# A residual encoder block on one core: x arrives transposed from the host, and the RMS roots are applied behind the projections

## The chip, the cores and the metric

One Trainium2 chip, one core. The time is device microseconds of one execution of the whole kernel. Before the change three runs took 2588.66, 2595.15 and 2600.83 us, median 2595.15 us. One further execution was profiled; all rows come from that one.

## What is computed

x has 2048 rows (frames) of 1024 channels, in f32. The part that matters here is the head of the layer:

```
n = x * rsqrt(mean(x*x, axis=-1) + 1e-6) * g_mix
z = n @ w_in + b_in          # columns: q | k | v | u | B | C | gate_attn | gate_conv
```

q, k and v (512 columns each, 8 heads of 64) go into a chunked attention with a per-head RMS norm; u, B and C go into a short causal convolution; the two gates scale the projections of both. The sum goes through `w_o` and is added to x. Then come a mixture of 32 experts and a gated embedding, which the change does not touch.

The root `r = rsqrt(mean(x*x) + 1e-6)` is one number for each row of x, and `g_mix` one for each channel. So `n @ W` is also `r * (x @ (g_mix * W))`.

## The kernel before, in words

Every matmul runs in three products: each operand is split into a high part (fp32r, a cast on ACT) and a low part (the difference, on DVE or POOL), and `mm3` (L85) issues high x high, high x low and low x high (L93, L94, L95). The helper `split` (L81) is the cast at L82 and the subtraction at L83. `split_scaled` (L479) does the same for `scale * raw`: ACT's scaled copy at L484, DVE's scalar_tensor_tensor at L485.

**Stage 1** (`stage1`, L130) makes q, k, v and the attention. It has 32 tiles of projection work: g = 0 and 1 (four heads each) times t = 0 to 15 (128 rows each). For each g the eight chunks of `w_in` (128x768 each, `load_w`, L163) are loaded and split once. A tile is worked on in three steps:

- `fetch` (L198) issues on SP's queue the load of the tile into `xt` (three buffers): from x for g = 0, from the DRAM buffer `NTd` for g = 1.
- `pre` (L209) makes the stationary operand `nh`, `nl`, that is the normalised tile with its channels on the partitions. For g = 0 it squares the tile on ACT (L219), makes the root on POOL (`rstd`, L126 and L127), multiplies by root and `gmix` on DVE (L222), turns the tile with eight 128x128 transposes on PE (L227) into two PSUM banks, copies them to `nraw` on ACT (L233), stores `nraw` to `NTd` (SP's queue, L234) and splits it (L238 on ACT, L239 on POOL, or on DVE for the first NV = 4 tiles). For g = 1 the turned tile comes back from `NTd` and is only split.
- `proj` (L242) is a generator of pieces: 24 matmuls of 512 columns into one bank (q and k), 24 of 256 columns into another (v), the bias added on DVE out of PSUM (L255, L274), the per-head norm, and the transposes of k and q (L290, L297).

The attention units (one head of one row tile: `score`, `turn`, `scale`, `pv`) are laid between those pieces by a loop written out by hand (L405 to L429): one piece of projection, one unit. `lead=11` pieces run before the first unit. `load_nb` (L184) loads a bias table for each head of g (`nbias`, five buffers).

**Stage 2** (`stage2`, L495) begins inside that loop when the projection pieces are used up, and runs its first pieces between the last attention units. It works in four blocks of 512 rows. For a block `load_n` (L545) brings eight slices of `NTd` (128x512 each) on ACT's queue into `nraw` (two buffers) and splits each into `nh`, `nl` (eight buffers): DMA, ACT cast (L82), DVE subtraction (L83). These are the moving operand of `conv` (u, C, B) and `gate`; weights come in chunks of 128x1024 through `chunk` (L487), split two chunks ahead. `out_proj` ends the block. The blocks after the first load their slices while `out_proj` of the block before runs.

The order of instructions on each engine is fixed when the kernel is built: the framework puts them in order by a simulated schedule, within the priorities of the program text.

Of the kernel before, what the change touches and what calls it, by code (L numbers as in the profile page):

```python
# [18 lines left out]
S = 2048  # L19
D = 1024  # L20
# [52 lines left out]
def bcast_rows(ap_row, n=128):  # L73
    return bass.AP(tensor=ap_row.tensor, offset=ap_row.offset, ap=[[0, n]] + [list(x) for x in ap_row.ap])


class K:
# [21 lines left out]
    def setup(self, ctx):  # L99
        tc, nc, a = self.tc, self.nc, self.a  # L100
        self.cst = c = ctx.enter_context(tc.tile_pool(name="cst", bufs=1))
        self.dr = d = ctx.enter_context(tc.tile_pool(name="dr", bufs=1, space=DRAM))
        self.ident = c.tile([128, 128], F32, name="ident")
        make_identity(nc, self.ident)
        self.identr = c.tile([128, 128], F32R, name="identr")
        nc.vector.tensor_copy(self.identr, self.ident)
        self.H = d.tile([S, D], F32, name="H")
        self.N2 = d.tile([S, D], F32, name="N2")
        self.Y = d.tile([2 * S + (NE + MAXOV) * CAP, D], F32, name="Y")
        self.PP = d.tile([S, D], F32, name="PP")  # L110
        self.mhalf = c.tile([128, 8], F32, name="mhalf")
        nc.vector.memset(self.mhalf, -0.5)
        self.NTd = d.tile([128, 8, S], F32, name="NTd")
        self.YAT = d.tile([128, 4, S], F32, name="YAT")
        self.banks, self.nbank = [], 0

        c.tile([128, 24], F32, name="pad")
# [12 lines left out]
    def stage1(self, outer, after, lead=11, lag=2):  # L130
        tc, nc, a = self.tc, self.nc, self.a
        with ExitStack() as ctx:
# [4 lines left out]
            pj = pjx.enter_context(tc.tile_pool(name="s1proj", bufs=2, side="right", reuse_waits="tile"))  # L137

            bank = self.bank
            gmix = pj.tile([128, D], F32, name="gmix", bufs=1)  # L140
            gqk = pj.tile([128, 8, HD], F32, name="gqk", bufs=1)
            gq = pj.tile([128, 2, HD], F32, name="gq", bufs=1)
            nc.scalar.dma_start(gmix, bcast_rows(a["g_mix"][0]))
            warm = pj.tile([128, 1], F32, name="ss")
            nc.scalar.activation(warm, self.mhalf[:, 0:1], AF.Square)


            early = att.tile([128, 4, 1024], F32, name="KT", bufs=1)
            early_n = att.tile([128, 6, 256], F32, name="PTh1", bufs=1)
            KT, PTh, PTl = [], [], []  # L150

            def tables():
# [5 lines left out]
                        nc.gpsimd.memset(p[:, 5, 0:128].bitcast(F32), 0.0)  # L158
                        P.append(p)

            W, NB, BQ, NS, QT, V, X, YT = {}, {}, {}, {}, {}, {}, {}, {}

            def load_w(g, ks):  # L163
                b = a["w_in"]
                for k in ks:
                    if g == 0:
                        raw = early[:, k - 4, 0:768] if k > 3 else att.tile([128, D], F32, name="QT", bufs=4)[:, 0:768]
                    else:
                        raw = pj.tile([128, D], F32, name="xt", bufs=3)[:, 0:768]
                    self.wlast = nc.sync.dma_start(raw.rearrange("p (s c) -> p s c", c=256),  # L170
                                      bass.AP(tensor=b.tensor, offset=b.offset + k * 128 * 5120 + g * 256,
                                              ap=[[5120, 128], [512, 3], [1, 256]]))
                    wh = pj.tile([128, 768], F32R, name="wh", bufs=8)
                    wl = pj.tile([128, 768], F32R, name="wl", bufs=8)
                    self.split(raw, wh, wl)
                    W[g, k] = (wh, wl)

            def load_bias(g):
# [4 lines left out]

            def load_nb(g, h):  # L184
                E = a["rel_ext"]
                nb = att.tile([128, 640], F32, name="nbias", bufs=5)
                with tc.issue_after(self.wlast.ins):
                    nc.sync.dma_start(nb, E[4 * g + h])
                if g == 0:
# [7 lines left out]

            def fetch(g, t):  # L198
                x = pj.tile([128, D], F32, name="xt", bufs=3)
                if g == 0:  # L200
                    nc.sync.dma_start(x, a["x"][0, t * 128:(t + 1) * 128, :])
                else:
                    nc.sync.dma_start(x.rearrange("p (k c) -> p k c", c=128), self.NTd[:, :, t * 128:(t + 1) * 128])
                X[g, t] = x

            def pool(g, t):
                return nc.vector if g == 0 and t < NV else nc.gpsimd

            def pre(g, t):  # L209
                x = X.pop((g, t))  # L210
                nh = pj.tile([128, 8, 128], F32R, name="nh")
                nl = pj.tile([128, 8, 128], F32R, name="nl")
                if g == 0:
                    if t == 0:
                        nraw = early_n[:, 0:4, :].rearrange("p a (b c) -> p (a b) c", c=128)
                    else:
                        nraw = pj.tile([128, 8, 128], F32, name="nraw", bufs=1)
                    ss = pj.tile([128, 1], F32, name="ss")
                    nc.scalar.activation(nl.rearrange("p a b -> p (a b)"), x, AF.Square, accum_out=ss)  # L219
                    rr = pj.tile([128, 1], F32, name="rr")  # L220
                    self.rstd(rr, ss, D)
                    nc.vector.scalar_tensor_tensor(x, x, rr, gmix, op0=ALU.mult, op1=ALU.mult)  # L222
                    for hf in range(2):
                        tp = bank()
                        for k in range(4):
                            kk = 4 * hf + k
                            nc.tensor.transpose(tp[:, k * 128:(k + 1) * 128], x[:, kk * 128:(kk + 1) * 128], self.ident)  # L227
                        sl = slice(4 * hf, 4 * hf + 4)
                        if t == 0:
                            tv = tp.rearrange("p (k c) -> p k c", c=128)  # L230
                            nc.scalar.copy(nh[:, sl], tv)  # L231
                            nc.vector.tensor_sub(nl[:, sl], tv, nh[:, sl].bitcast(F32))  # L232
                        nc.scalar.copy(nraw[:, sl, :], tp)  # L233
                    nc.sync.dma_start(self.NTd[:, :, t * 128:(t + 1) * 128], nraw)  # L234
                else:
                    nraw = x.rearrange("p (k c) -> p k c", c=128)
                if g or t:
                    nc.scalar.copy(nh, nraw)  # L238
                    pool(g, t).tensor_tensor(nl, nraw, nh.bitcast(F32), op=ALU.subtract)  # L239
                NS[g, t] = [(nh[:, k, :], nl[:, k, :]) for k in range(8)]  # L240

            def proj(g, t):  # L242
# [4 lines left out]
                for half in range(2):  # L247
# [4 lines left out]
                    if half == 0:  # L252
                        yield
                zqk = pj.tile([128, 8, HD], F32, name="zqk", bufs=3)
                nc.vector.tensor_add(zqk, pqk.rearrange("p (h d) -> p h d", d=HD),  # L255
                                     BQ[g][:, 0:2, :].rearrange("p s (h d) -> p (s h) d", d=HD))
                sqk = pj.tile([128, 8, HD], F32, name="sqk")
                pool(g, t).tensor_tensor(sqk, zqk, zqk, op=ALU.mult)
                yield
# [11 lines left out]
                pool(g, t).tensor_tensor(zg, zn, gqk, op=ALU.mult)  # L271
                yield
                zv = pj.tile([128, 4, HD], F32, name="zv", bufs=1)
                nc.vector.tensor_add(zv, pv[:, 0:256].rearrange("p (h d) -> p h d", d=HD),  # L274
                                     BQ[g][:, 2, :].rearrange("p (h d) -> p h d", d=HD))
                Vt = att.tile([128, 4, 2, HD], F32R, name="Vt", bufs=8)
                V[g, t] = Vt
                nc.scalar.copy(Vt[:, :, 0, :], zv)
# [24 lines left out]
            def pieces():  # L303
                fetch(*tiles[0])
                load_w(0, range(WX))
                fetch(*tiles[1])
                load_w(0, range(WX, 8))
                load_bias(0)
                nc.sync.dma_start(gq[:, 0], bcast_rows(a["g_q"][0]))
                nc.sync.dma_start(gq[:, 1], bcast_rows(a["g_k"][0]))  # L310
# [7 lines left out]
                while n < 4 * len(tiles) or live:  # L318
# [5 lines left out]
                            live.remove(p)  # L324
                    if r == 0 and i + 2 < len(tiles):
                        fetch(*tiles[i + 2])
                    if r == 1 and i + 1 < len(tiles):
                        pre(*tiles[i + 1])
                    n += 1
# [165 lines left out]
    def stage2(self, outer, inner):  # L495
# [30 lines left out]
        with ExitStack() as ctx:  # L526
# [12 lines left out]
            tr = rt.tile([128, 512], F32, name="nraw")  # L539
            nc.scalar.dma_start(tr[:, 0:256], a["tri"])  # L540
            nc.gpsimd.tensor_copy(self.tri, tr[:, 0:256])
            halo = small[:, 44:52].rearrange("p (c j) -> p c j", j=2)
            nc.gpsimd.memset(halo, 0.0)

            def load_n(b):  # L545
                out = []
                for k in range(8):
                    raw = rt.tile([128, 512], F32, name="nraw")
                    nc.scalar.dma_start(raw, self.NTd[:, k, 512 * b:512 * b + 512])
                    hi = rt.tile([128, 512], F32R, name="nh", bufs=8)  # L550
                    lo = rt.tile([128, 512], F32R, name="nl", bufs=8)
                    self.split(raw, hi, lo)
                    out.append((hi, lo))
                return out
# [918 lines left out]
def layout(inputs):  # L1473
# [3 lines left out]

    w13 = np.stack([np.asarray(inputs[n])[0].reshape(NE, 8, 128, 4, 128) for n in ("w1", "w3")])
    arrays["w13"] = np.ascontiguousarray(w13.transpose(1, 4, 0, 3, 2, 5)).reshape(NE, 1024, 1024)
    arrays["cst"] = constants()  # L1480
    arrays["tri"] = triangle()
    return arrays
# [15 lines left out]
```

## Time and profile before

| what | value |
|---|---|
| median of three runs | 2595.15 us (2588.66 to 2600.83) |
| the profiled execution | 2593.1 us, of which its span is 2591.3 us |
| mean granted TensorE clock | 0.992 of full speed |
| stage 1 | from 0 to about 560 us |
| stage 2 | from about 560 us to about 1540 us (first and last block overlap their neighbours) |

The 1.8 us between the profiled time and its span lie outside what the profile shows. The profiled execution is 2.05 us below the median of the runs.

### The profile page before, as it was taken

What the parts mean: (1) busy time and instruction counts of PE and PEld (TensorE: products, weight loads), DVE (VectorE), ACT (ScalarE), POOL (GpSimd) and SP (SyncE); (2) the same over time, 40 slices, a digit from 0 to 9 for tenths busy, and PEclk for the clock granted to TensorE, in tenths of its full rate; (3) what the DMA queues carried; (4) which work ended last, traced back from release to release, by engine and by line L of the source; (5) the groups of instructions that cost most, each with busy time, mean ns of one, the idle gap of its engine ahead of it and who ended that gap; (6) DMA issues with size and microseconds to landing.
All of it is one profiled execution on the core that took longest, in us unless ns stands there. A gap on an engine that the chain in (4) does not pass through costs nothing.

```text
span 2591.3 us, 38162 instructions
## 1 busy us (share of the span) xinstructions
PE 2530.0 (98%) x13933; PEld 2191.1 (85%) x13933; DVE 1709.1 (66%) x2745; ACT 1348.1 (52%) x2188; POOL 557.9 (22%) x568
## 2 busy tenths in 40 slices
PE   7999999999999999999999999999999999998998
PEld 6888888888888888888888887998989898986887
DVE  7788867786445444544444445788889888886544
ACT  5666655664333333333333233677777777775322
POOL 2566465520000010001000001111111111111222
PEclk9999999999999999999999999999999999999999
DMA  5212311033536333533353344789999989998452
GB/s 190 73 54 72 109 51 41 14 95 104 154 95 204 120 98 110 199 112 93 121 184 109 98 148 167 267 315 338 324 321 335 335 317 337 335 336 290 157 182 101
DMA packets 331168, 460.47 MB, mean 178 GB/s; under 512 B 26352, under 2 KB 222192, under 8 KB 330976
## 3 DMA queue, kind: packets, MB, share of 16 engines
q1 hardware_dynamic: 297536, 388.35, 45.0%
q0 software_dynamic: 11040, 38.21, 3.9%
q10 hardware_dynamic: 22400, 31.42, 3.7%
q8 instruction: 111, 1.82, 0.3%
q14 instruction: 81, 0.66, 0.1%
HBM read 397.93 MB, written 60.00 MB: 177 GB/s over the span
## 4 chain that ended last, share of the span: by engine, by line
PE 89%; DVE 5%; DMA 3%; ACT 1%; issue 1%; POOL 1%; SPq 0%; ACTq 0%; POOLq 0%; DVEq 0%
PE acc L93 21%; PE acc L95 21%; PE acc L94 21%; PE acc L1079 8%; PE acc L1080 3%; PE acc L1151 2%; PE big L351 2%; PE big L381 2%; PE acc L394 1%; PE acc L395 1%; PE acc L685 1%; PE acc L1049 1%; DMA wraw<-w 1%; DMA h<-H 1%; PE acc L297 1%
## 5 line engine op out<-in xcount | busy, mean ns | idle before, releaser
L83 DVE TENSOR_TENSOR wlo<-wraw,whi 128x1024 fp32r<-128x1024 f32 x560 | 717.0, 1285 | 398.4 <-ACT whi L82 385.3
L82 ACT CAST whi<-wraw 128x1024 fp32r<-128x1024 f32 x560 | 588.5, 1053 | 742.0 <-PE acc L94 376.8
L93 PE MATMUL acc<-nh,whi 128*128 128x512 f32 x896 | 349.8, 392 | 1.9 <-ACT nh L82 1.9
L94 PE MATMUL acc<-nl,whi 128*128 128x512 f32 x896 | 350.0, 391 | 0.0
L95 PE MATMUL acc<-nh,wlo 128*128 128x512 f32 x896 | 348.8, 389 | 0.0
L1079 PE MATMUL acc<-x,whi 128*128 128x320 f32 (+5 forms) x1088 | 289.2, 351 | 1.4 <-DVE x L1062 1.4
L1080 PE MATMUL acc<-x,wlo 128*128 128x160 f32 (+5 forms) x1088 | 258.8, 238 | 0.0
L1080 PEld LDWEIGHTS acc<-x,wlo 128*128 128x128 f32 x1088 | 209.7, 193 | 0.1
L1079 PEld LDWEIGHTS acc<-x,whi 128*128 128x128 f32 x1088 | 206.0, 189 | 1.8 <-DVE x L1062 1.5
L93 PEld LDWEIGHTS acc<-nh,whi 128*128 128x128 f32 x896 | 168.1, 188 | 37.0 <-ACT nh L82 2.6
L95 PEld LDWEIGHTS acc<-nh,wlo 128*128 128x128 f32 x896 | 168.3, 188 | 34.5
L94 PEld LDWEIGHTS acc<-nl,whi 128*128 128x128 f32 x896 | 168.4, 188 | 33.4
L94 PE MATMUL acc<-wl,nh 128*128 128x256 f32 (+1 forms) x512 | 174.5, 342 | 2.5 <-DVE wl L83 2.5
L93 PE MATMUL acc<-wh,nh 128*128 128x512 f32 (+1 forms) x512 | 176.8, 346 | 0.0
L95 PE MATMUL acc<-wh,nl 128*128 128x256 f32 (+1 forms) x512 | 175.2, 343 | 0.0
L610 POOL TENSOR_TENSOR sa<-sa,sc 128x512 f32<-128x512 f32 x32 | 41.2, 1288 | 538.3 <-DVE sc L609 493.3
L386 ACT CAST PTh<-big 128x640 fp32r<-128x640 f32 (+4 forms) x128 | 80.3, 627 | 87.5 <-PE big L381 86.2
L369 ACT ACTIVATE L<-L,four 128x640 f32<-128x640 f32 (+4 forms) x128 | 98.4, 769 | 37.8 <-DVE four L368 15.1
L387 DVE TENSOR_TENSOR PTl<-big,PTh 128x640 fp32r<-128x640 f32 (+4 forms) x128 | 94.0, 735 | 27.6 <-ACT PTh L386 27.1
L94 PEld LDWEIGHTS acc<-wl,nh 128*128 128x128 f32 x512 | 98.5, 192 | 12.4 <-DVE wl L83 3.5
L95 PEld LDWEIGHTS acc<-wh,nl 128*128 128x128 f32 x512 | 98.3, 192 | 9.9 <-DVE nl L232 0.2
L93 PEld LDWEIGHTS acc<-wh,nh 128*128 128x128 f32 x512 | 98.5, 193 | 8.6 <-ACT nh L231 0.2
(329 smaller groups left out, 5691.8 us busy)
## 6 DMA issues: line engine op xcount, KB each, us to landing
wraw<-w SPq DMA_DIRECT2D x384, 512.0 KB, 5.3
wraw<-w_in SPq DMA_DIRECT2D x112, 512.0 KB, 3.7
wraw<-w_o SPq DMA_DIRECT2D x32, 512.0 KB, 3.6
y<-Y SPq DMA_DIRECT2D x32, 512.0 KB, 4.3
xt<-x SPq DMA_DIRECT2D x16, 512.0 KB, 3.8
xt<-NTd SPq DMA_DIRECT2D x16, 512.0 KB, 4.1
nraw<-NTd ACTq DMA_DIRECT2D x32, 256.0 KB, 3.8
wraw<-w_pa SPq DMA_DIRECT2D x32, 256.0 KB, 2.7
```

The source lines that it names most:

```text
L82: (hi_eng or self.nc.scalar.copy)(hi, raw)
L83: (lo_eng or self.nc.vector).tensor_sub(lo, raw, hi.bitcast(F32))
L93: self.nc.tensor.matmul(ps, sh, mh, start=first, stop=False)
L94: self.nc.tensor.matmul(ps, sh, ml, start=False, stop=False)
L95: mm = self.nc.tensor.matmul(ps, sl, mh, start=False, stop=last)
L351: nc.tensor.matmul(big[:, 512 * c:512 * c + hi - lo], QT[g, t][:, s, h * 128:(h + 1) * 128], KT[0][:, h, ks:ks + hi - lo], start=(s == 0), ...
L369: nc.scalar.activation(L[:, :n], L[:, :n], AF.Exp, bias=mn, scale=-1.0, accum_out=sm)
L381: nc.tensor.transpose(pt[:, j * 128:(j + 1) * 128], L[:, j * 128:(j + 1) * 128], self.ident)
L386: nc.scalar.copy(hi, ptv)
L387: nc.vector.tensor_sub(lo, ptv, hi.bitcast(F32))
L1079: nc.tensor.matmul(p[:, 0:2 * c], hi[:, sl], x[:, k, 0:2 * c], start=(k == 0), stop=False)
L1080: nc.tensor.matmul(p[:, 0:c], lo[:, sl], x[:, k, 0:c], start=False, stop=(k == 7))
```

## The change

The host passes one more array, `xT`: x turned, as [128, 8, 2048] (channel within its group of 128, group, row). The kernel gets these edits:

- **No normalised copy in DRAM.** `NTd` goes; a DRAM row `RD` [1, 2048] for the roots comes.
- **g_mix goes into the weights of stage 1.** Instead of the broadcast `gmix` (128x1024) a tile `gT` [128, 8] is loaded element by element (ACT's queue), and each chunk of `w_in` is split by `split_scaled` with its column of `gT`.
- **Tiles come in turned.** `fetch` reads `xT` for both g. `pre` splits what was loaded at once, with nothing before it: no multiplication (L222), no transposes (L227), no copies (L233), no store (L234).
- **The roots are made beside it.** For g = 0 a second load (`fetch_rows`, SP's queue, two buffers `xr`) brings the tile in rows; ACT squares it, POOL makes the root into a column of the tile `R`, and SP's queue stores the column to `RD`.
- **The roots are applied behind the products.** At L255 and L274 the addition of the bias becomes a scalar_tensor_tensor: product times root plus bias.
- **Stage 2 normalises its own slices.** `load_n` loads for each block a broadcast `rb` (128x512) of `RD` on ACT's queue and multiplies each slice of `xT` by `g_mix` (a column of `gmT`, loaded once on ACT's queue) and `rb`, with a scalar_tensor_tensor on DVE between the DMA and the cast.
- `nbias` has four buffers instead of five.

```diff
-        self.NTd = d.tile([128, 8, S], F32, name="NTd")
+        self.RD = d.tile([1, S], F32, name="RD")
...
-            gmix = pj.tile([128, D], F32, name="gmix", bufs=1)
+            gT = pj.tile([128, 8], F32, name="gT", bufs=1)
+            R = pj.tile([128, 16], F32, name="R", bufs=1)
...
-            nc.scalar.dma_start(gmix, bcast_rows(a["g_mix"][0]))
+            nc.scalar.dma_start(gT, a["g_mix"][0].rearrange("(k p) -> p k", p=128))
...
-                    self.split(raw, wh, wl)
+                    self.split_scaled(raw, wh, wl, gT[:, k:k + 1])
...
-                nb = att.tile([128, 640], F32, name="nbias", bufs=5)
+                nb = att.tile([128, 640], F32, name="nbias", bufs=4)
...
             def fetch(g, t):
                 x = pj.tile([128, D], F32, name="xt", bufs=3)
-                if g == 0:
-                    nc.sync.dma_start(x, a["x"][0, t * 128:(t + 1) * 128, :])
-                else:
-                    nc.sync.dma_start(x.rearrange("p (k c) -> p k c", c=128), self.NTd[:, :, t * 128:(t + 1) * 128])
+                nc.sync.dma_start(x.rearrange("p (k c) -> p k c", c=128), a["xT"][:, :, t * 128:(t + 1) * 128])
                 X[g, t] = x
+
+            def fetch_rows(t):
+                XR[t] = pj.tile([128, D], F32, name="xr", bufs=2)
+                nc.sync.dma_start(XR[t], a["x"][0, t * 128:(t + 1) * 128, :])
...
             def pre(g, t):
-                x = X.pop((g, t))
+                xv = X.pop((g, t)).rearrange("p (k c) -> p k c", c=128)
                 nh = pj.tile([128, 8, 128], F32R, name="nh")
                 nl = pj.tile([128, 8, 128], F32R, name="nl")
+                n = 4 if (g, t) == (0, 0) else 8
+                for k in range(0, 8, n):
+                    nc.scalar.copy(nh[:, k:k + n], xv[:, k:k + n])
+                    pool(g, t).tensor_tensor(nl[:, k:k + n], xv[:, k:k + n], nh[:, k:k + n].bitcast(F32), op=ALU.subtract)
                 if g == 0:
+                    xr = XR.pop(t)
                     ss = pj.tile([128, 1], F32, name="ss")
-                    nc.scalar.activation(nl.rearrange("p a b -> p (a b)"), x, AF.Square, accum_out=ss)
-                    rr = pj.tile([128, 1], F32, name="rr")
-                    self.rstd(rr, ss, D)
-                    nc.vector.scalar_tensor_tensor(x, x, rr, gmix, op0=ALU.mult, op1=ALU.mult)
-                    for hf in range(2):
...
-                    nc.sync.dma_start(self.NTd[:, :, t * 128:(t + 1) * 128], nraw)
...
+                    nc.scalar.activation(xr, xr, AF.Square, accum_out=ss)
+                    self.rstd(R[:, t:t + 1], ss, D)
+                    nc.sync.dma_start(self.RD[0:1, 128 * t:128 * t + 128].rearrange("o t -> t o"), R[:, t:t + 1])
...
-                nc.vector.tensor_add(zqk, pqk.rearrange("p (h d) -> p h d", d=HD),
-                                     BQ[g][:, 0:2, :].rearrange("p s (h d) -> p (s h) d", d=HD))
+                nc.vector.scalar_tensor_tensor(zqk, pqk.rearrange("p (h d) -> p h d", d=HD), R[:, t:t + 1],
+                                               BQ[g][:, 0:2, :].rearrange("p s (h d) -> p (s h) d", d=HD), op0=ALU.mult, op1=ALU.add)
...
                 fetch(*tiles[0])
                 load_w(0, range(WX))
+                fetch_rows(0)
                 fetch(*tiles[1])
                 load_w(0, range(WX, 8))
+                fetch_rows(1)
...
                         fetch(*tiles[i + 2])
+                        if i + 2 < NT:
+                            fetch_rows(i + 2)
...
+            gmT = small[:, 52:60]
+            nc.scalar.dma_start(gmT, a["g_mix"][0].rearrange("(k p) -> p k", p=128))
...
             def load_n(b):
+
                 out = []
+                rb = rt.tile([128, 512], F32, name="rb", bufs=1)
+                nc.scalar.dma_start(rb, self.RD[0:1, 512 * b:512 * b + 512].to_broadcast([128, 512]))
                 for k in range(8):
                     raw = rt.tile([128, 512], F32, name="nraw")
-                    nc.scalar.dma_start(raw, self.NTd[:, k, 512 * b:512 * b + 512])
+                    nc.scalar.dma_start(raw, a["xT"][:, k, 512 * b:512 * b + 512])
+                    nc.vector.scalar_tensor_tensor(raw, raw, gmT[:, k:k + 1], rb, op0=ALU.mult, op1=ALU.mult)
```

L274 changes as L255 does. `split_scaled`, which was there before, is:

```python
        nc.scalar.activation(hi, raw, AF.Copy, scale=scale)
        nc.vector.scalar_tensor_tensor(lo, raw, scale, hi.bitcast(F32), op0=ALU.mult, op1=ALU.subtract)
```

## Rows read from the trace of the kernel before

**Rows 1.** The page's head and its busy times by engine.

```profile
span 2591.3 us, 38162 instructions
...
PE 2530.0 (98%) x13933; PEld 2191.1 (85%) x13933; DVE 1709.1 (66%) x2745; ACT 1348.1 (52%) x2188; POOL 557.9 (22%) x568
```

**Rows 2.** Stretches: length; busy us (count) PE, PEld, DVE, ACT, POOL; clock; DMA.

```profile
100.00:200.00 100.00, 97.69 (x700) 90.79 (x700) 81.25 (x149) 66.77 (x134) 62.12 (x57) 1.00 0.23 69
...
600.00:700.00 100.00, 100.00 (x483) 84.12 (x481) 52.63 (x81) 39.90 (x57) 2.58 (x2) 1.00 0.43 127
```

**Rows 3.** The same view: tiles 5 to 15 of g = 0, then of g = 1.

```profile
88.48:264.00 175.52, 170.91 (x1205) 156.37 (x1203) 143.87 (x286) 118.25 (x238) 107.29 (x98) 1.00 0.23 68
370.40:540.61 170.21, 164.47 (x1134) 149.22 (x1133) 127.94 (x286) 99.81 (x205) 92.58 (x78) 1.00 0.09 27
```

**Rows 4.** Groups of instructions by line in the stretch from 88.48 to 264.00 us.

```profile
L222 DVE SCALAR_TENSOR_TENSOR xt<-xt,rr,gmix 128x1024 f32<-128x1024 f32 x9 | 12.0, 1336 | 1.9 <-POOL rr L127 1.8
L233 ACT COPY nraw<-acc 128x512 f32<-128x512 f32 x20 | 11.8, 615 | 0.0
...
L227 PE MATMUL acc<-ident,xt 128*128 128x128 f32 x80 | 11.2, 275 | 0.0
```

**Rows 5.** The chain of waits from 88.5 to 264 us, shares by line.

```profile
by line: PE acc L95 14.0%; PE acc L93 13.4%; PE acc L94 13.3%; PE big L351 11.4%; PE big L381 9.8%; PE acc L394 5.4%; PE acc L395 5.4%; PE acc L227 4.3%; DVE sqk L269 3.8%; DVE L L374 3.7%; PE acc L297 3.6%; DVE PTl L387 2.0%; DVE L L362 1.
```

**Rows 6.** Timeline of the start: start us, length us, engine, line, operation, idle before.

```profile
5.96 1.06 ACT L219 ACTIVATE nl<-xt 128x1024 fp32r<-128x1024 f32 x1 [3.30 <-DMA xt<-x]
...
7.48 0.83 ACT L82 CAST wh<-QT 128x768 fp32r<-128x768 f32 x1 [0.37 <-DMA QT<-w_in]
...
9.40 1.97 PE L227 MATMUL acc<-ident,xt 128*128 128x128 f32 x8 [9.40 <-DVE xt L222]
...
11.19 0.79 PE L93 MATMUL acc<-wh,nh 128*128 128x512 f32 x1
...
18.57 0.85 ACT L82 CAST wh<-KT 128x768 fp32r<-128x768 f32 x1
...
19.79 0.95 DVE L83 TENSOR_TENSOR wl<-KT,wh 128x768 fp32r<-128x768 f32 x1
```

**Rows 7.** DMA issues: tile, queue, count, KB each, median us to landing.

```profile
KT<-w_in SPq DMA_DIRECT2D x4, 384.0 KB, 8.2
...
gple<-g_ple ACTq DMA_DIRECT2D x1, 4.0 KB, 3.7
...
misc<-g_ffn ACTq DMA_DIRECT2D x1, 4.0 KB, 6.8
```

**Rows 8.** Lines 484 and 485 (scaled split): shortest/median/longest ns.

```profile
L484 ACT ACTIVATE whi<-wraw,gple x7: 1137/1142/1155, 2351.6 to 2381.5; 128x1024 fp32r<-128x1024 f32 x7
...
L485 DVE SCALAR_TENSOR_TENSOR wlo<-wraw,gple,whi x7: 1272/1283/1758, 2352.7 to 2383.3; 128x1024 fp32r<-128x1024 f32 x7
```

**Rows 9.** Groups by line and shape, 0 to 700 us: two DVE forms out of PSUM.

```profile
L255 DVE TENSOR_TENSOR zqk<-acc,bqkv 128x512 f32<-128x512 f32 x32 | 22.0, 686 | 11.4 <-PE acc L95 11.1
...
L583 DVE SCALAR_TENSOR_TENSOR z<-acc,small,u 128x512 f32<-128x512 f32 x4 | 3.0, 751 | 8.4 <-PE acc L95 8.4
```

**Rows 10.** Groups by line from 564 to 592 us, where stage 2 begins.

```profile
L93 PE MATMUL acc<-nh,whi 128*128 128x512 f32 x24 | 8.3, 399 | 1.9 <-ACT nh L82 1.9
...
L83 DVE TENSOR_TENSOR nl<-nraw,nh 128x512 fp32r<-128x512 f32 x8 | 5.5, 686 | 4.8 <-ACT nh L82 4.7
```

**Rows 11.** Timeline of ACT and its queue in the same stretch.

```profile
578.62 1.66 ACTq L549 DMA_DIRECT2D nraw<-NTd  x2
...
582.78 1.66 ACTq L549 DMA_DIRECT2D nraw<-NTd  x2
```

**Rows 12.** Block 1: ACT's last slices, and PE's first matmul on them.

```profile
792.26 1.22 ACT L82 CAST nh<-nraw 128x512 fp32r<-128x512 f32 x2 [1.25 <-DMA nraw<-NTd]
...
827.84 0.39 PE L93 MATMUL acc<-nh,whi 128*128 128x512 f32 x1
```

More of the change, by code (lines that the diff above doesn't have):

```diff
@@ L148, in stage1 @@
             early = att.tile([128, 4, 1024], F32, name="KT", bufs=1)
-            early_n = att.tile([128, 6, 256], F32, name="PTh1", bufs=1)
             KT, PTh, PTl = [], [], []
@@ L159, in tables @@
                         P.append(p)
-            W, NB, BQ, NS, QT, V, X, YT = {}, {}, {}, {}, {}, {}, {}, {}
+            W, NB, BQ, NS, QT, V, X, XR, YT = {}, {}, {}, {}, {}, {}, {}, {}, {}
             def load_w(g, ks):
@@ L213, in pre @@
                 if g == 0:
[L214 to L217, printed above, removed]
+                    xr = XR.pop(t)
                     ss = pj.tile([128, 1], F32, name="ss")
-                    nc.scalar.activation(nl.rearrange("p a b -> p (a b)"), x, AF.Square, accum_out=ss)
-                    rr = pj.tile([128, 1], F32, name="rr")
@@ L221, in pre @@
-                    self.rstd(rr, ss, D)
-                    nc.vector.scalar_tensor_tensor(x, x, rr, gmix, op0=ALU.mult, op1=ALU.mult)
-                    for hf in range(2):
[L224 to L233, printed above, removed]
@@ L234, in pre @@
-                    nc.sync.dma_start(self.NTd[:, :, t * 128:(t + 1) * 128], nraw)
[L235 to L239, printed above, removed]
+                    nc.scalar.activation(xr, xr, AF.Square, accum_out=ss)
+                    self.rstd(R[:, t:t + 1], ss, D)
+                    nc.sync.dma_start(self.RD[0:1, 128 * t:128 * t + 128].rearrange("o t -> t o"), R[:, t:t + 1])
@@ L273, in proj @@
                 zv = pj.tile([128, 4, HD], F32, name="zv", bufs=1)
-                nc.vector.tensor_add(zv, pv[:, 0:256].rearrange("p (h d) -> p h d", d=HD),
-                                     BQ[g][:, 2, :].rearrange("p (h d) -> p h d", d=HD))
+                nc.vector.scalar_tensor_tensor(zv, pv[:, 0:256].rearrange("p (h d) -> p h d", d=HD), R[:, t:t + 1],
+                                               BQ[g][:, 2, :].rearrange("p (h d) -> p h d", d=HD), op0=ALU.mult, op1=ALU.add)
                 Vt = att.tile([128, 4, 2, HD], F32R, name="Vt", bufs=8)
@@ L1479, in layout @@
     arrays["w13"] = np.ascontiguousarray(w13.transpose(1, 4, 0, 3, 2, 5)).reshape(NE, 1024, 1024)
+    arrays["xT"] = np.ascontiguousarray(np.asarray(inputs["x"])[0].T.reshape(8, 128, S).transpose(1, 0, 2))
     arrays["cst"] = constants()
```

## The prediction

> **What bounds the kernel now.** I read the page's busy times first: PE is busy for 2530.0 of 2591.3 us, DVE for 1709.1 [rows 1]. So about 61 us of the whole span are left in which PE shows nothing, and a change that moves the end must take work off PE or close a gap. The view by stretches then says where the gaps are: from 600 to 700 us PE is busy for all of 100.00 us with DVE at 52.63; from 100 to 200 us PE is at 97.69 with DVE at 81.25 and POOL at 62.12 [rows 2]. The reader is to see two regimes. In stage 2 PE alone counts, and DVE has half its time to spare. In stage 1 PE is still the longest, but chains through DVE, POOL and ACT end some of the waits.
>
> The third view prices the change almost by itself. Tiles 5 to 15 of g = 0 and of g = 1 run the same projection beside the same number of attention pieces; the g = 1 tiles have no square, root, multiplication by `gmix`, transposes or `nraw` copies. Ten tiles took 175.52 us for g = 0 and 170.21 us for g = 1, with 1205 and 1134 PE instructions [rows 3]. After the change a g = 0 tile is a g = 1 tile plus a square and a root.
>
> **Stage 1, per tile of g = 0.** Removed from PE: eight transposes. Ten tiles of them keep PE busy for 11.2 us [rows 4], and the chain of waits, which counts each moment once, has 4.3% of 175.5 us, 7.5 us, on them [rows 5]. Removed from DVE: one multiplication of 1.34 us a tile; from ACT: two copies of 0.615 us [rows 4]. Kept: the square on ACT (1.06 us at 5.96 [rows 6]) and the root on POOL. SP's queue loses the `NTd` store and gains a load of rows and a store of 128 roots; the row load has two buffers and is asked for two tiles ahead, so its landing is covered by a tile of about 17 us. The root is needed only at L255, several pieces after `pre`. If that cover went, the wait would sit on DVE ahead of the attention's work.
>
> What reaches the end? 80 transposes less would leave 1125 instructions in the first stretch against 1134 in the second, which thus did nine more, at 170.91/1205 = 0.14 us each 1.3 us [rows 3]. The like-for-like gain is (175.52 - 170.21 + 1.3)/10 = 0.66 us a tile; without that correction it is 0.53, and if all the transposes' busy time went, 1.12. I take 0.6, since the square and the root stay, near the pair of stretches because that measures the end and not one engine. 16 tiles: **-9.6 us**, bounds -8.5 and -17.9.
>
> **The start.** Today the first projection matmul runs at 11.19 us, behind square, root, multiplication, transposes (9.40) and a copy [rows 6]. Then nothing is in front of it but x's landing at 5.96, a cast, and the first weight chunk, which is there at 7.48 and takes 0.83 on ACT [rows 6] and about 0.96 on DVE (1.283 for 1024 columns [rows 8]): 9.3 us. That is 2 us sooner. The end of the phase moves by less: the eighth chunk's low part is done at 19.79 + 0.95 [rows 6], and the last chunks land 8.2 us after they are asked for [rows 7]; `fetch_rows(0)` puts 512 KB in front of them while the 512 KB of `gmix` go. I take **-2**, bounds 0 and -3.
>
> One new thing stands in front of all weights: `gT`, 4 KB in pieces of 4 bytes on ACT's queue. The nearest rows are the two loads of the same form, landing in 3.7 and 6.8 us [rows 7]. Asked for in the first microsecond, it is there at 4.7 to 7.8 us, about when the first chunk is. Cost 0, covered by that chunk's landing; with the 8.2 us of the slowest row it would be there at 9.2, and 1.7 us of the 2 are lost.
>
> The Trainium skill, DMA: Bandwidth & Descriptors, "Rules for kernel authors", speaks against this edit: a load with a non-contiguous last dimension becomes one descriptor per element, here 1,024 for `gT`. By that rule the load is slow for its size, and the trace agrees: 4 KB took as long as larger loads do [rows 7].
>
> **Edits near nothing.** L255 becomes a scalar_tensor_tensor: 751 against 686 ns [rows 9], 32 times 0.065 = 2.1 us on DVE, and L274 by analogy about half; hidden by PE's matmuls, 0, at worst 3. Weights by `split_scaled`: per 1024 columns 1.142 us on ACT and 1.283 on DVE [rows 8], so 0.86 and 0.96 for 768, against 0.83 and 0.95 [rows 6]: 0.04 us for each of 16 chunks, 0. `nbias` with four buffers: the first table of g = 1 waits for the last unit that reads head 0's, some six units before it is needed; 0, at worst one landing, 4 us, since the unit behind it waits for its table.
>
> **The beginning of stage 2.** Here the change adds a wait. Block 0's slices are loaded as PE comes to use them: PE waits 1.9 us for `nh` [rows 10], and pairs of loads go out 4.2 us apart, each when the pair before is split and its buffers free [rows 11]. Now each slice first passes DVE for about 0.75 us (the same form at 751 ns [rows 9]). In a pair, two multiplications and two subtractions of 0.686 us [rows 10] follow one another on DVE, while the casts run between them: some 0.9 us more a pair, 3.6 for four pairs, plus `rb` and `gmT` ahead on ACT's queue, about 1. Behind the waiting multiplications stand DVE's attention work and weight splits; PE has attention units to do meanwhile. Bounds: 0 (they cover it) and 5 (all of it shows). I take **+3**.
>
> **Blocks 1 to 3.** 24 multiplications, 24 x 0.75 = 18 us of DVE. The last slices of block 1 are cast by 793.5 us, and PE first needs them at 827.84 [rows 12]: 34 us of cover, while DVE is busy for half the time [rows 2]. Cost 0.
>
> **The sum** against the profiled execution of 2593.1 us (span 2591.3): -9.6 - 2 + 3 = -8.6, 2584.5. The median of the runs lies 2.05 us above the profiled one, so 2586.5; I say **2586**.
>
> **Rivals.**
>
> *All of PE's share comes back.* Stage 1's DVE work also falls by 1.34 us a tile, and the multiplication had two SBUF operands while POOL worked beside it. For it: in the g = 0 stretch DVE is at 143.87 of 175.52 us, in the g = 1 stretch at 127.94 of 170.21 [rows 3], and the chain has 3.8% on L269 and 3.7% on L374 [rows 5]. Against it: the g = 1 stretch had this relief and is already in the 0.66. Transposes and freed waits together at 0.9 to 1.0 a tile (15), start 3, and stage 2's beginning covered: 2595.15 - 18 = 2577. If POOL gained as much as DVE, 16 x 1.34 = 21 in place of the 15, it would be 2571; I give that end 0.05 of this rival's chance.
>
> The Trainium skill, SBUF — State Buffer, "SBUF: two separate sides", says that a DVE instruction with two SBUF inputs and a POOL instruction that reads SBUF exclude one another for their whole length. By that rule taking out 16 such instructions frees POOL as well as DVE. The trace agrees a little: the multiplication took 1.336 us on average beside POOL's work, and the scaled split of the same size 1.283 [rows 4, 8].
>
> *Chains hide the gain.* PE's eight transposes fill waits for DVE and POOL. For it: 3.8% and 3.7% of the chain on DVE [rows 5]. Half of 9.6, start 1, stage 2 +3: 2592.
>
> *Slower: DVE holds up stage 2.* The multiplication waits on DVE, in order, for its slice's DMA, with the weights' subtractions behind it. If PE then waits for weights in every block, all 32 are exposed, 32 x 0.75 = 24 us, and some of the 1.25 us that ACT now waits for a pair [rows 12] passes to DVE, say 5 us over 16 pairs: 29 against -11.6, 2612. It decides once the wait is longer than the two chunks of weights split ahead, 48 matmuls at 100/483 us [rows 2], 10 us. For it: PE already waits for slices where stage 2 begins [rows 10]; against it: the 34 us.
>
> *The start is not freed.* `gT` lands late and the first matmul stays at 11 us: 2588.5, inside the range.
>
> **How the numbers follow.** 0.5% is 13 us, about what a measurement of this kernel can tell from no change. Forecast 0.47 (its own range 2579 to 2592: the bounds of its terms, without the far end of the transposes), all of PE's share 0.27, hidden 0.11, slower 0.10, start not freed 0.05. Faster by over 13 us, below 2582: the second and 0.07 of the first, 0.34. Slower, above 2608: 0.10. The rest 0.56. The range from 2573 to 2603 takes in the first three and leaves out the slower case and the far end of the second.
>
> **What would show it.** No L227 and no `nraw` copies in stage 1; the stretch from tile 5 to 15 of g = 0 at about 170 us; the first matmul of L93 near 9 us; PE waiting some 3 us more for `nh` between 560 and 595 us; stage 2 with PE at 100% after that. I am wrong if the g = 0 tiles keep their 17.6 us, if L83's `wlo` appears among PE's waits in stage 2, or if the projection waits for roots.

## The result and the profile after

The changed kernel takes 2635.01 us (median of four runs, 2633.25 to 2636.31) against 2593.07 us for the kernel before on the same chip: a ratio of 1.0158, 95% interval 1.0143 to 1.0174. It is slower by some 42 us, where 2586 us with a range of 2573 to 2603 was forecast.

The page's head, its busy times and three of its slices rows (40 equal slices of 65.8 us):

```profile
span 2633.5 us, 37897 instructions
...
PE 2530.9 (96%) x13805; PEld 2187.5 (83%) x13805; DVE 1700.9 (65%) x2761; ACT 1334.2 (51%) x2156; POOL 561.9 (21%) x568
...
PE   4699999998999999999999999999999999998998
...
PEclk7799999999999999999999999999999999999999
DMA  9611221105534533453353334799989998997553
```

PE has lost the 128 transposes (13933 matmuls in [rows 1], 13805 here), yet it is busy for as long as before, since many of those left ran at a lower clock (0.76 from 0 to 129.07 us; 0.94 in the kernel before from 0 to 88.48, up to the same tile), and the span is 42.2 us longer. The slices say where: in the first one PE is at 4 tenths, the DMA engines at 9, and the granted clock is at 0.7 in the first two. Stretches of the changed kernel (columns as in [rows 2]); the last two are tiles 5 to 15 of g = 0 and of g = 1:

```profile
20.00:60.00 40.00, 18.30 (x96) 15.62 (x94) 13.65 (x25) 11.64 (x21) 9.97 (x23) 0.72 1.02 157
60.00:100.00 40.00, 21.90 (x107) 19.30 (x106) 13.29 (x37) 15.09 (x34) 12.17 (x19) 0.67 0.89 110
...
129.07:298.70 169.63, 164.64 (x1136) 149.58 (x1134) 128.44 (x286) 100.89 (x206) 95.18 (x79) 1.00 0.13 38
405.93:575.03 169.10, 164.82 (x1133) 149.29 (x1131) 130.15 (x286) 99.72 (x204) 92.47 (x78) 1.00 0.09 27
```

The first two of them in the kernel before:

```profile
20.00:60.00 40.00, 37.59 (x241) 33.74 (x240) 30.79 (x65) 21.23 (x46) 12.29 (x25) 0.96 0.40 130
60.00:100.00 40.00, 35.61 (x214) 30.82 (x213) 29.94 (x69) 25.76 (x63) 22.19 (x22) 0.91 0.23 73
```

From 20 to 100 us PE is busy for 40.2 us in place of 73.2, at a clock of about 0.7 (a mix of its two levels, 1.2 and 2.4 GHz), while the DMA engines are 89 to 102% busy (the share adds up the time of packets and can pass 100%) and move only 110 to 157 GB/s. After that the kernel does what was forecast: ten tiles of g = 0 take 169.63 us, against 175.52 in [rows 3]. The loss arises at the front: `zqk` of tile 5 comes at 129.07 us instead of 88.48 (+40.6), tile 15 at 298.70 instead of 264.00 (+34.7).

What does the front wait for? Seven pieces of the chain of waits of the changed kernel from 0 to 130 us (start, length, what; L221 is the square):

```profile
23.80 14.70 DMA xr<-x
38.58 1.16 ACT xr L221 x2
40.09 1.14 ACT xr L221 x2
41.43 14.98 DMA xr<-x
56.49 1.15 ACT xr L221 x2
57.67 13.81 DMA xr<-x
71.56 1.16 ACT xr L221 x2
```

Load of rows, square, load of rows, square: the chain is ACT waiting for `xr`. The view of that tile, then of `RD`; the landing times of the second are those of the 16 stores and of stage 2's four loads of `rb` together:

```profile
L221 ACT ACTIVATE xr<-xr x16: 1056/1057/1076, 11.5 to 109.0; 128x1024 f32<-128x1024 f32 x16
...
  DMA xr<-x: 45.7, 12
...
DMA to landing us min/median/max: 5.4/9.5/15.0
```

```profile
L223 SPq DMA_DIRECT2D RD<-R x16: 320/330/3397, 21.3 to 111.4; - x16
...
DMA to landing us min/median/max: 3.4/12.5/15.0
```

Two things are to be seen. All 16 squares run in the first 110 us, although tile 15's products come at 298.70: when the kernel was built they were put ahead in ACT's order. And a store of 128 roots, 512 bytes, takes 13.0 us to land (the median of the 16 alone, in the DMA view below), longer than the row loads of 512 KB beside it (10.0). So 16 row loads, 16 stores and the tiles' own loads are packed into some 90 us, and ACT, which works in order, stands at 12 of the 16 squares, 45.7 us in all. PE waits behind ACT and DVE (PE's waits from 0 to 130 us: total, times, longest):

```profile
PE acc L274 <- DVE zk L266: 23.2, 3, 11.2
PE acc L93 <- ACT KT L276: 12.1, 1, 12.1
```

The DMA view from 20 to 130 us: the queue's packets with the share of 16 engines' time that they took, and two issues with their landing times:

```profile
q1 hardware_dynamic: 12440, 12.46, 77.8%
...
xr<-x SPq DMA_DIRECT2D x14, 512.0 KB, 10.0
...
RD<-R SPq DMA_DIRECT2D x16, 0.5 KB, 13.0
```

### The profile page after: what moved, and what is told of

Same layout as the page of the kernel before. It is cut to its first block, busy times and chain, and to the rows that moved or that the text cites. A ratio compares the mean times of both kernels' runs of the same rounds, so it can differ in the third digit from the quotient of the medians.

```text
span 2633.5 us, 37897 instructions
## 1 busy us (share of the span) xinstructions
PE 2530.9 (96%) x13805; PEld 2187.5 (83%) x13805; DVE 1700.9 (65%) x2761; ACT 1334.2 (51%) x2156; POOL 561.9 (21%) x568
## 4 chain that ended last, share of the span: by engine, by line
PE 87%; DMA 5%; DVE 4%; ACT 2%; issue 1%; POOL 0%; SPq 0%; ACTq 0%; POOLq 0%; DVEq 0%
PE acc L93 21%; PE acc L94 21%; PE acc L95 21%; PE acc L1073 8%; PE acc L1074 3%; DMA xr<-x 3%; PE acc L1145 2%; PE big L339 2%; PE big L369 2%; PE acc L382 1%; PE acc L383 1%; PE acc L679 1%; PE acc L1043 1%; DVE PTl L375 1%; DMA wraw<-w 1%
## 5 line engine op out<-in xcount | busy, mean ns | idle before, releaser
L94 PE MATMUL acc<-wl,nh 128*128 128x512 f32 (+1 forms) x512 | 177.8, 347 | 3.4 <-DVE wl L473 3.3
L95 PE MATMUL acc<-wh,nl 128*128 128x512 f32 (+1 forms) x512 | 177.6, 347 | 0.0
L604 POOL TENSOR_TENSOR sa<-sa,sc 128x512 f32<-128x512 f32 x32 | 42.2, 1318 | 541.4 <-DVE sc L603 541.4
L95 PEld LDWEIGHTS acc<-wh,nl 128*128 128x128 f32 x512 | 101.4, 198 | 10.2
```

What stands on the lines that cost most here:

```text
L94: self.nc.tensor.matmul(ps, sh, ml, start=False, stop=False)
L95: mm = self.nc.tensor.matmul(ps, sl, mh, start=False, stop=last)
```

## The experiments

Eleven kernels ran. All edits are against the changed kernel unless it is said otherwise, and each median stands beside the ratio to the kernel before on the same chip.

**e1, e2, e3, e4: which property of the store costs the time.** e1 takes the stores out:

```diff
-nc.sync.dma_start(self.RD[0:1, 128 * t:128 * t + 128].rearrange("o t -> t o"), R[:, t:t + 1])
-nc.scalar.dma_start(rb, self.RD[0:1, 512 * b:512 * b + 512].to_broadcast([128, 512]))
+nc.scalar.dma_start(rb, bcast_rows(a["g_mix"][0, 0:512]))
```

> Edit: the sixteen stores of the roots to RD are left out, and rb is loaded as a broadcast of g_mix instead (so stage 2 multiplies by wrong roots; the work is the same). ACT's order, with its squares ahead, is kept. Theory 1 (the 4-byte stores hold SP's queue and the DMA engines, the row loads behind them land late, and ACT waits in order): the row loads land in 4 to 7 us, tile 5's zqk starts near 88 to 92 us instead of 129, the time is 2590 to 2600. Theory 2 (the squares and row loads run ahead of the tiles and stall ACT by themselves, store or not): the time stays above 2615.

e2 keeps the stores and ties each square to its own tile:

```diff
+cast = nc.scalar.copy(nh[:, k:k + n], xv[:, k:k + n])
+with tc.issue_after(cast.ins):
     nc.scalar.activation(xr, xr, AF.Square, accum_out=ss)
```

> Edit: the stores stay; each square is ordered behind the cast of its own tile on ACT, so the squares, the row loads and the stores come at the tiles' pace. Theory 1: each store still takes about 12 us to land, but what stands behind it on SP's queue is not needed for another tile, so most of the loss goes: 2593 to 2605. Theory 2: the same or better, 2590 to 2600. Theory 3 (a store in flight holds back every other DMA, the weights' and tiles' too, whatever the order): above 2615.

e3 keeps the order and the pieces, and changes their addresses (`rb` as in e1):

```diff
-self.RD = d.tile([1, S], F32, name="RD")
+self.RD = d.tile([S, 128], F32, name="RD")
-nc.sync.dma_start(self.RD[0:1, 128 * t:128 * t + 128].rearrange("o t -> t o"), R[:, t:t + 1])
+nc.sync.dma_start(self.RD[128 * t:128 * t + 128, 0:1], R[:, t:t + 1])
```

> Edit: the stores stay as many and as small (128 pieces of 4 bytes each), but each root goes to its own 512-byte row of a larger RD; rb is loaded as a broadcast of g_mix (wrong roots, same work). ACT's order is kept. If the stores are slow because 128 pieces go to one 512-byte stretch of DRAM: a store lands in 3 to 4 us and the time is 2590 to 2602. If any 4-byte store is slow: landing stays near 12 us and the time near 2630.

e4 turns the 16 columns of roots once, behind tile 15, and stores them as 16 rows of 512 bytes:

```diff
+if t == NT - 1:
+    tr = bank()
+    nc.tensor.transpose(tr[0:16, 0:128], R, self.ident)
+    RT = pj.tile([16, 128], F32, name="RT", bufs=1)
+    nc.vector.tensor_copy(RT, tr[0:16, 0:128])
+    nc.sync.dma_start(self.RD.rearrange("o (t p) -> (o t) p", p=128), RT)
```

> Edit: the roots stay in SBUF; after tile 15 one transpose on PE turns the 128x16 roots into 16x128, DVE copies them, and one DMA of 16 rows of 512 bytes stores them. ACT's order is kept, the result is the reference's. Theory 1: as without stores, 2590 to 2600. Theory 2: above 2615.

| run | median us | ratio, 95% interval | ACT waits for `xr`, 0 to 130 us | queue's DMA time, 20 to 130 us |
|---|---|---|---|---|
| changed kernel | 2635.01 | 1.0158 (1.0143 to 1.0174) | 45.7 us | 77.8% |
| e1 no store | 2592.28 | 0.9997 (0.9987 to 1.0006) | 8.6 us | 39.8% |
| e2 squares held back | 2597.42 | 1.0009 (0.9997 to 1.0021) | 0.8 us | 42.0% |
| e3 roots 512 bytes apart | 2588.56 | 0.9983 (0.9972 to 0.9993) | 8.2 us | 41.2% |
| e4 one turned store | 2591.23 | 0.9997 (0.9983 to 1.0011) | 7.5 us | 39.9% |

The table's last column is that of SP's queue; e2's 42.0% holds nine stores and fewer loads than the others (11.46 MB). e1's line is

```profile
q1 hardware_dynamic: 12613, 13.95, 39.8%
```

Without the stores the loss is gone, and the squares still run ahead (the last one at 68 us): running ahead is harmless by itself. With the stores but at the tiles' pace, some 37 of the 42 us are gone: the store is nearly harmless by itself. (Theories 1 and 2 of e2 both allowed this time; it is the third that falls.) It takes both. And e3 writes as many 4-byte pieces as the change, closer together (its stores go out from 21.5 to 70.6 us, the change's from 21.3 to 111.4), and costs nothing. How long its stores take to land, the trace does not say. The DMA view from 20 to 130 us of e3 (all packets with their sizes, then the queue):

```profile
DMA packets 15099, 14.18 MB, mean 129 GB/s; under 512 B 2780, under 2 KB 12784, under 8 KB 15088
...
q1 hardware_dynamic: 15088, 14.05, 41.2%
```

Over the 110 us and 16 engines, 77.8% less the 39.8% of e1 is 669 us of engine time more for 16 stores, 42 us each; e3's 41.2% leaves 25 us, 1.5 each. These are estimates: the loads that fall into the 110 us are not quite the same (12.46, 13.95 and 14.05 MB). The number of small pieces is the same; that they lie side by side in DRAM makes them some 27 times as dear. The Trainium skill, DMA: Bandwidth & Descriptors, "Specifications", says that a transfer under 512 bytes is a read-modify-write and stays below line rate. By size alone e3 and the change would cost the same; the traces show that size alone does not decide.

**e5: is it SP's queue or the engines?** The store goes to ACT's queue:

```diff
-nc.sync.dma_start(self.RD[0:1, 128 * t:128 * t + 128].rearrange("o t -> t o"), R[:, t:t + 1])
+nc.scalar.dma_start(self.RD[0:1, 128 * t:128 * t + 128].rearrange("o t -> t o"), R[:, t:t + 1])
```

> The change as it is, but each tile's store of 128 roots is issued on ACT's DMA queue, and the row loads stay on SP's. Theory Q (the row loads are late because they stand behind the stores in SP's queue): the row loads land in some 5 us again, the stores still take some 12 us but nobody waits for them; 2590 to 2605 us (the stores held to their tiles gave 2597). Theory E (the stores fill the 16 DMA engines themselves, whichever queue they come from: these were over 89% busy at 110 to 157 GB/s between 20 and 100 us): the row loads are as late as in the change, 2620 to 2640 us. In both, ACT waits for each root before it issues (about 1.1 us of POOL behind the square), at most 16 x 1.1 = 18 us of ACT, which has idle time from 20 to 100 us.

2639.14 us, ratio 1.0173 (1.0156 to 1.0190): theory E. (The profiled execution took 2651.84 us, the longest of the five.) The DMA view of e5 from 20 to 130 us (q1 is SP's queue, q10 ACT's), then ACT's waits from 60 to 130 us:

```profile
q1 hardware_dynamic: 8866, 11.81, 85.3%
q10 hardware_dynamic: 2304, 0.01, 4.3%
```

```profile
ACT xr L221 <- DMA xr<-x: 46.6, 7, 8.4
```

The stores are now in q10 and show 4.3%, 76 us or some 5 for each store. The loads in q1, which have nothing of the stores in their queue any more, take more engine time than in the change, and over twice that of e1 for fewer bytes. Their packets wait in the engines. So most of the 42 us is not time of the store's own packets. It is the same in the changed kernel: summed over the packets of 20 to 130 us, the 1,792 of 4,096 bytes (the rows of the 14 row loads) took 917 us there and 352 in e1, those of 4 bytes 137 and 4. The Trainium skill, DMA: Bandwidth & Descriptors, "Issuing engines are not separate DMA queues", says that DMAs of all issuing engines run on the same 16 engines; the trace agrees.

**e6: how far apart is enough?** Against e3:

```diff
-self.RD = d.tile([S, 128], F32, name="RD")
+self.RD = d.tile([S, 16], F32, name="RD")
```

> As the spread store, but with the roots 64 bytes apart (16 floats) in place of 512; stage 2 multiplies by g_mix's first 512 values in place of the roots, so its products are other numbers at the same cost. If pieces hinder each other that lie within one stretch of 512 bytes, 8 roots share each one and the store stays slow: between the spread store (2588.6 us) and the change (2635 us), 2600 to 2635. If they hinder each other only within 64 bytes or less, it is as fast as the spread store: 2586 to 2592 us, with the DMA engines' time of 20 to 130 us near 41% as there, not 78%.

2591.83 us, ratio 0.9996 (0.9987 to 1.0006), the queue at 42.1%: 64 bytes apart is enough. Neither e3 nor e6 reads the spread roots back, so what that would cost is not shown. The border lies between 4 and 64 bytes; nothing finer was tried.

**e7: the store alone, in the kernel before.**

```diff
 self.rstd(rr, ss, D)
+nc.sync.dma_start(self.RD[0:1, 128 * t:128 * t + 128].rearrange("o t -> t o"), rr)
```

> The kernel before with one thing added: each tile's 128 roots are stored as 128 pieces of 4 bytes into one row of DRAM, on SP's queue, and nobody reads them. Each square there comes at the pace of its tile. Theory (the store takes 12 us or so by itself, and costs time only where loads that are needed soon stand behind it): the stores land in 10 to 14 us, the DMA share of 20 to 130 us goes up from 30% by some 25 points, but the time rises by 0 to 8 us only, 2593 to 2602 (keeping the stores at the tiles' pace cost the change 6 us: 2597.4 against 2591.2). Rival (the piecewise store costs its tile 2 us or more wherever it stands, by 16 stores): 2625 us or more.

2596.62 us, ratio 1.0011 (1.0001 to 1.0020): 3 us. The queue's DMA time from 20 to 130 us goes from 29.9 to 44.7% with eight stores in it, 15 points and not the 25 expected, 33 us of engine time for each: nearly as dear as in the change, and nearly hidden, since the loads behind it are asked for two tiles ahead and the work comes tile by tile. That is the cover that the prediction had counted on.

**e8: why the start gains nothing.** With the stores repaired (e4), tile 5's `zqk` comes at 88.62 us, where 88.48 was before. The first matmul is indeed earlier, at 7.43 us against 11.19 [rows 6]. The timeline of e4's DVE, tile 0 and its `zk`, and PE's waits from 0 to 60 us:

```profile
23.70 0.75 DVE L244 SCALAR_TENSOR_TENSOR zqk<-acc,R,bqkv 128x512 f32<-128x512 f32 x1 [3.71 <-PE acc L95]
...
32.25 0.42 DVE L271 TENSOR_TENSOR zk<-zqk,zk 128x256 fp32r<-128x256 f32 x1
```

```profile
PE acc L279 <- DVE zk L271: 8.4, 1, 8.4
```

Tile 1 is now ready early too, and PE was given the products of tiles 0 and 1 in turns, so that both end at 24 us. Then PE has nothing in front of tile 0's transposes and waits for the norm. e8 is e4 with one order more:

```diff
+with (tc.issue_after(self.t0.ins) if (g, t) == (0, 1) else contextlib.nullcontext()):
     self.mm3(pqk, st[4 * half:4 * half + 4], [(W[g, k][0][:, 0:512], W[g, k][1][:, 0:512]) for k in ks], 4 * half, 8)
...
-self.mm3(pv[:, 0:256], st[4:8], [(W[g, k][0][:, 512:768], W[g, k][1][:, 512:768]) for k in range(4, 8)], 4, 8)
+mm = self.mm3(pv[:, 0:256], st[4:8], [(W[g, k][0][:, 512:768], W[g, k][1][:, 512:768]) for k in range(4, 8)], 4, 8)
+if (g, t) == (0, 0):
+    self.t0 = mm
```

> The change with the one turned store (2591.2 us), and on PE the products of tile 1 for q and k are ordered behind the last product of tile 0. Theory (the start gains nothing because PE interleaves tile 0 and tile 1, so tile 0's last product comes at 23.9 us although the first comes at 7.4, and PE then waits 8.4 us for tile 0's zk): tile 0's zqk comes at about 20 to 21 us (its last wl is there at 18.8) in place of 23.7, PE's wait for zk falls to 3 to 5 us, and the time falls by 2 to 4 us, to 2587 to 2589. Rival (the start is bound by what follows, DVE's own queue of nl, bias blocks and zqk, or the arrival of bias and tables): zqk moves, but the first KT and the tiles behind do not, 2590.5 to 2592 us.

2585.49 us, ratio 0.9971 (0.9959 to 0.9984). Tile 0's `zqk` and PE's wait moved as the theory said, and the time fell somewhat further than it said. Of the versions that leave nothing out, this one and the two that build on it (e10, e11) are faster than the kernel before. The same two views of e8, the first with tile 5's `zqk`:

```profile
20.65 0.75 DVE L246 SCALAR_TENSOR_TENSOR zqk<-acc,R,bqkv 128x512 f32<-128x512 f32 x1
...
82.61 0.75 DVE L246 SCALAR_TENSOR_TENSOR zqk<-acc,R,bqkv 128x512 f32<-128x512 f32 x1 [0.92 <-PE acc L96]
```

```profile
PE acc L283 <- DVE zk L275: 3.8, 1, 3.8
```

**e9: what the multiplications of stage 2 cost.** Against e8, in `load_n`:

```diff
-nc.vector.scalar_tensor_tensor(raw, raw, gmT[:, k:k + 1], rb, op0=ALU.mult, op1=ALU.mult)
```

> The version with the turned store and tile 0 first (2585.5 us), with stage 2's multiplication by root and g_mix left out in all four blocks (32 instructions of 750 ns on DVE), so its products are other numbers at the same cost. From the last zqk (10.2 us ahead of the kernel before) to the first yh cast of block 0 (7.1 us ahead) that version loses 3.1 us. Theory M (block 0's eight multiplications, 6.0 us of DVE, hold up the beginning of stage 2, as the prediction had it): the yh cast comes some 3 us earlier, at about 641 us, and the time falls to 2581 to 2583.5. Rival (PE shows no wait for nh there, so they are covered and the 3 us are lost to something else, the loads of xT into two buffers or a clock fall): the cast stays at 643 to 644.5 and the time at 2584.5 to 2587.

2590.14 us, ratio 0.9988 (0.9979 to 0.9998): not faster, if anything slower than e8. The last `zqk` comes at 528.13 us, even earlier than in e8, but the first `yh` cast of block 0 at 647.04 instead of 643.96, and PE has a wait that e8 has not (PE's waits of e9 from 530 to 700 us, then ACT's from 550 to 650 us):

```profile
PE acc L94 <- ACT nh L83: 6.8, 1, 6.8
```

```profile
ACT nh L83 <- DMA nraw<-xT: 7.0, 2, 3.6
ACT L L366 <- DMA rb<-RD: 6.2, 2, 3.7
```

The last line is a cost of the edit itself. With the multiplications gone nothing reads `rb`, so all four of its loads go out between 553.0 and 566.9 us, one after another into the one buffer, and ACT, which issues them, stands still for 6.2 us (in e8 one load of `rb` goes out there, at 555.5, and the next at 587.5). The third slice is asked for at 567.23 us, behind the last of them; its cast, at 572.85, ends PE's wait. So e9 takes 6 us of DVE out and puts other waits in: it bears out neither theory M nor the rival, which both expected the cast by 644.5 us, and does not decide between them.

**e10, e11: e8 with e2's order as well, and e8 with half of the multiplications on POOL.**

```diff
+if k % 2:
+    nc.gpsimd.tensor_tensor(raw, raw, rb, op=ALU.mult)
+    nc.gpsimd.tensor_scalar(raw, raw, gmT[:, k:k + 1], None, op0=ALU.mult)
+else:
     nc.vector.scalar_tensor_tensor(raw, raw, gmT[:, k:k + 1], rb, op0=ALU.mult, op1=ALU.mult)
```

> The version with the turned store and tile 0 first (2585.5 us), and on ACT each tile's square is ordered behind that tile's cast. In that version all 16 squares run ahead, in the first 110 us. Theory (with the stores gone the row loads land in time, and where the squares stand no longer matters): 2584 to 2587 us. Rival (16 x 1.3 us of squares packed into 100 us of ACT hold up the softmax of the first tiles: PE waits for PTh 3.1 us before 130 us): 2581.5 to 2584.

> The version with the turned store and tile 0 first (2585.5 us), with every second multiplication of stage 2 on POOL, in two instructions (128x512: root, then g_mix; about 1.3 and 1 us, POOL being idle from 560 to 660 us), and the other four of a block on DVE. If the multiplications on DVE hold up block 0, half of them gone saves about half of what leaving all out saves: 2583 to 2585. If POOL's 2.3 us make a longer chain than DVE's 0.75 between a load and its cast, with two buffers for the loads, the casts come later: 2586 to 2590, with PE waiting for nh.

2587.13 us, 0.9975 (0.9966 to 0.9983), and 2586.43 us, 0.9974 (0.9964 to 0.9983). Neither can be told from e8. Once the store is cheap, where the squares stand makes no difference that these runs can tell. On POOL the two instructions took 1.40 and 2.16 us on average from 540 to 700 us, longer than expected, and PE waited 1.2 us for `nh`, as the second case said (in e8 it did not wait for it). For the time the runs decide nothing, since the effects looked for are as small as the intervals.

## Why the prediction was wrong

**The step that failed** is the sentence on SP's queue under "Stage 1, per tile of g = 0": "SP's queue loses the `NTd` store and gains a load of rows and a store of 128 roots; the row load has two buffers and is asked for two tiles ahead, so its landing is covered by a tile of about 17 us." It was wrong twice over.

- The store was named and then not priced. Its 512 bytes go out in 128 pieces of 4 bytes into one row, land in 13.0 us and add 42 us of DMA engine time, most of it in the packets of the loads beside it (e1 and e5 against the change). No row of before showed such a store, so it needed bounds from both sides. The nearest rows were the piecewise loads of 4 KB, 3.7 and 6.8 us [rows 7]. The rule that the prediction cites from the Trainium skill, DMA: Bandwidth & Descriptors, "Rules for kernel authors" (one descriptor per element) was weighed against `gT`, which landed in 2.9 us and cost nothing, and not against the store, which goes out element by element too.
- The cover of 17 us holds only if the square comes with its tile. Nothing tied it there: a square needs its rows and a buffer, so the order built for ACT took all 16 within 110 us, and the rows were then needed as soon as they could land. At the tiles' pace the cover is real (e2: +6 us against e4; e7: +3 us in the kernel before).

Of the rivals, "slower" had the right sign for a wrong reason: DVE and stage 2 played no part. The prediction also had the wait in another place: it would "sit on DVE", and the sign named was that "the projection waits for roots". In the changed kernel DVE's L239, which takes the root, waits 3.5 us from 0 to 130 us, and for PE; the wait is one step earlier and on another engine, ACT at the square, 45.7 us for `xr`, and what stands behind it in ACT's order (`nh`, `KT`, the softmax) is what DVE and PE then wait for.

**The other terms**, read from the changed kernel and from e8, in which the store does not hide them:

- *0.6 us a tile of g = 0: right.* 175.52 less 169.63 is 5.89 over ten tiles. The last `zqk` of stage 1 in e8 is 10.2 us ahead of before (540.61 and 530.42), where tiles and start together had 11.6.
- *The start, -2: the sum was right only with an order that the change does not have.* In e4, five tiles at 0.59 us should have put tile 5 at 85.5; it came at 88.62, so the start cost 3.1. In e8 tile 5 is 5.87 us ahead, of which the start is 2.9. The first matmul, forecast at 9.3 us, came at 7.38 in the changed kernel: high times high needs no low part, so the 0.96 us of DVE did not belong in that term. What was missed is the work behind: PE's first wait moved to tile 0's `zk`.
- *`gT` at 0: right* (2.9 us to landing). *L255 at 751 ns: right* (743). The splits took 0.94 and 1.02 us, against 0.86 and 0.96: a small miss, covered.
- *The beginning of stage 2, +3: the size fits, the cause is not shown.* From the last `zqk` to the first `yh` cast e8 loses 3.1 of its 10.2 us:

```profile
530.42 0.74 DVE L246 SCALAR_TENSOR_TENSOR zqk<-acc,R,bqkv 128x512 f32<-128x512 f32 x1
...
562.30 0.62 PE L94 MATMUL acc<-nh,whi 128*128 128x512 f32 x2
...
643.96 0.62 ACT L83 CAST yh<-nraw 128x512 fp32r<-128x512 f32 x1 [0.67 <-issue]
```

(In the timeline of the kernel before these stand at 540.61, 569.89 and 651.06.) The forecast put the 3 us into PE's wait for `nh`. But PE shows no such wait in e8 from 530 to 700 us, where the kernel before had 1.9 us of it, and 2.6 of the 3.1 us are gone by PE's first product on `nh`, before which it did 192 instructions instead of 185. So the order of work around the last attention units is the likeliest place. Whether the multiplications brought it about stays open, since e9 changed more than them; that the term came out right in size is luck as far as the runs tell.
- *Blocks 1 to 3 at 0: right.* From that cast to the first square of the feed-forward part it is 677.8 us before and 677.9 in e8 (1328.88 and 1321.87).

The sum was a gain of 8.6 us. Against the kernel before on their chips e8, e10 and e11 gain 7.8, 5.3 and 6.0 us; the turned store alone (e4) gains 2.8, which its interval does not tell from nothing. So the sum comes near with two things that the change does not have, a cheap store and tile 0 first, and partly by luck. The change as it stands misses it by one 512-byte store a tile, made at squares that nothing ties to their tiles.

## What to carry to other kernels

Price every DMA that an edit adds by its pieces and by where they land, the small stores first: a column of single floats into consecutive addresses is better turned on chip and stored once (e4), or spread out, if reading it back spread is cheap, which was not tried. A cover of "one tile" is only one if an order ties the work to its tile; ask of every new instruction how early the builder may put it, and what stands behind it on an engine that works in order. When a start is freed, look for the next thing that the first tile waits for.

## What the runs showed of the hardware

Writes of 4 bytes to neighbouring addresses of DRAM hinder one another: 128 of them took 13.0 us to land, with row loads of 10.0 us in the same queue, and added an estimated 42 us of DMA engine time (77.8% against 39.8%); as many, 64 or 512 bytes apart, added an estimated 2.5 and 1.5 us (42.1 and 41.2%). Most of the 42 us is in packets of other loads, and of another queue's too (e5: 4.3% in the stores' queue, 85.3% in that of the loads). A load of 1,024 pieces of 4 bytes, `gT`, landed in 2.9 us at the start of the kernel: reads in pieces were not slow there. What in the memory makes the writes wait, and where between 4 and 64 bytes it ends, was not tried.
